# Mixer A's softmax weights of the second layer are turned by VectorE and a round trip through DRAM, and that layer's weights come in halves

## The chip, the cores and the metric

The kernel runs on one core of a Trainium2 chip. The metric is the device time in microseconds of one execution; the median of three runs is 2662.04 us.

## The reference

Two layers of a hybrid encoder over 256 tokens of 2048 channels, in float32. Each layer is, in short:

```python
mod = silu(c) @ ada_w[l] + ada_b[l]                  # six vectors of 2048: shift, scale, gate, twice
h = rmsnorm(x, norm_mix[l]) * (1 + sc_a) + sh_a
qa, ka, va, qb, kb, vb, ga, gb = split_cols(h @ w_in[l])
ya = window_attention(rot(norm(qa)), rot(norm(ka)), va, sink_a[l]) @ w_proj_a[l]   # mixer A, 8 heads
yb = neighbourhood_attention(norm(qb), norm(kb), vb, rel_bias_b[l]) @ w_proj_b[l]  # mixer B, 8 heads
x = x + gt_a * ((sigmoid(ga) * ya + sigmoid(gb) * yb) @ w_out[l])
h = rmsnorm(x, norm_ffn[l]) * (1 + sc_m) + sh_m
g, v = split(depthwise_conv(h @ w_up[l]), 2)
x = x + gt_m * ((silu(g) * v) @ w_down[l])
```

In both mixers a head's softmax weights are a 256 x 256 matrix p (queries by keys). The product with v contracts over the keys, so p has to be turned: keys on the partitions, queries along the row.

## The kernel before

All weights of a layer are one stream of 128 x 128 blocks in the order of their use. Sixteen blocks are a unit of 1 MB; a unit is loaded by SyncE into one of four `raw` tiles, which the modulation weights `aw` share. ScalarE casts each half of a unit to float32r (L336, the high part) and VectorE subtracts that from the original (L337, the low part), into one of four `hl` tiles. TensorE makes three matmuls of each block: high by high, high by low and low by high. `tokens` (L408) makes the q, k, v projections, with L418 to L420; `features` (L392) makes everything else, through `feature_block` (L355 to L357). The list `bg` of background jobs is advanced once at the end of each unit (`tick`, L264); a job has a rate in steps per unit.

The attention of both mixers is such a job (`attention`, L906), at `ATT[l]` steps a unit, and `ATT_B[l]` after mixer A's projection. At each step every live head moves on by one `yield`, and one new head starts if its q and k are there. A head's steps are: scores on TensorE (L648), row maximum, exponential and division on VectorE and ScalarE (L651 to L667); then p is turned and split into high and low parts pT (L430 on ScalarE, L431 on VectorE); then the product with v on TensorE (L697).

There are two ways to turn p. Where `rows` is None, TensorE makes four 128 x 128 transposes into PSUM (`tp`, L689). Otherwise `turned_blocks` (L308) lets VectorE turn each 32 x 32 block in place (L313), into q's and k's own room, and GpSimd's queue writes the blocks to a DRAM tile `pY` at their turned places, eight DMAs of 32 KB a head (L316). `later(BACK[...], back)` reads them back through SyncE's queue, two DMAs of 128 KB (L299), a number of units later, or when the job comes to pT, whichever is first; a read-back is also kept behind the last weight half that VectorE had been given (`BEHIND`). `MOVED[l]` says how many heads of mixer A and of mixer B go this second way: before, none in the first layer, and mixer B's eight in the second. The steps of GpSimd are otherwise the reciprocal roots of the q and k norms (`qrs`, L482) and of the layer norms.

`attended(HA)` runs mixer A's heads to their end before its projection. The instructions of each engine are put in order by a scheduler when the program is built; each engine, and each queue, then runs them in that order.

Of the kernel before, what the change touches and what calls it, by code (L numbers as in the profile page):

```python
# [9 lines left out]
F32 = mybir.dt.float32  # L10
# [5 lines left out]
P = 128  # L16
L = 2
D = 2048
S = 256
# [12 lines left out]
BLOCK = 32  # L32
# [47 lines left out]

H_RATE = [2.7, 1.7]

ATT = [1.288, 0.4]
ATT_B = [0.21, 0.4]

SCORES_3 = (1,)

BACK = [3, 4]
MOVED = [(0, 0), (0, 8)]

ADA_ORDER = [[p * KC + k for k in range(KC) for p in ps] for ps in ((0, 1), (2,), (3, 4), (5,))]
ADA_ORDER = [i for part in ADA_ORDER for i in part]
# [47 lines left out]
def encoder(ctx: ExitStack, tc: tile.TileContext, a: dict, out: bass.AP):  # L140
    nc = tc.nc
# [18 lines left out]
    dram = pool("dram", 2, space=bass.MemoryType.DRAM)  # L160
# [54 lines left out]
    def ada(l):  # L215

        mod = lay.tile([P, 96], F32, name=f"mod{l}", tag="mod")
        ab = load(a["ab"][l], [P, 96], f"ab{l}", lay, tag="ab", bufs=1)
        nrm = load(a["nrm"][l], [P, 2, KC], f"nrm{l}", lay, tag="nrm", bufs=1)
        amod = lay.tile([P, 2, KC], F32, name=f"amod{l}", tag="amod")  # L220
        mods[l], amods[l] = mod, amod
        for n, i in enumerate(ADA_ORDER):
            if l == 0 and n in OWN:
                if OWN[n] not in own:
                    own[OWN[n]] = [place(OWN[n], 16 if OWN[n] == "o" else 12, F32, f"aw_{OWN[n]}"), 0]
                t, k = own[OWN[n]]
                own[OWN[n]][1] += 1
                raw = t[:, KC // 2 * k : KC // 2 * (k + 1)].rearrange("p k s -> p (k s)")
            else:
                raw = rawp.tile([P, D], F32, name=f"aw{l}_{n}", tag="raw")  # L230
            nc.sync.dma_start(raw[:], a["aw"][l, n])
            nc.vector.tensor_tensor_reduce(  # L232
                out=raw[:], in0=raw[:], in1=cact[:], scale=1.0, scalar=ab[:, i : i + 1],
                op0=ALU.mult, op1=ALU.add, accum_out=mod[:, i : i + 1],
            )
            part, kc = divmod(i, KC)
            if part in (1, 4):
                w = part // 3
                nc.vector.scalar_tensor_tensor(
                    out=amod[:, w, kc : kc + 1], in0=mod[:, i : i + 1], scalar=1.0, in1=nrm[:, w, kc : kc + 1],  # L240
                    op0=ALU.add, op1=ALU.mult,
                )
            done[l] = n + 1
            yield
# [42 lines left out]
    def once(fn):  # L287
# [6 lines left out]

        return run

    def read_back(dst, src):

        tc.add_manual_dep(nc.sync.dma_start(dst, src).ins, halved[0], BEHIND)  # L299
# [7 lines left out]

    def turned_blocks(p, rows, n, tag):  # L308

        y = dram.tile([P, n, S], F32, name=tag, tag=tag)  # L310
        to = y[:].rearrange("(b i) n (t a j) -> t a i n b j", i=BLOCK, t=2, a=P // BLOCK)
        for t, row in enumerate(rows):
            nc.vector.transpose(out=row, in_=p[t])  # L313
            src = row.rearrange("p (n b j) -> p n b j", n=n, j=BLOCK)
            for a in range(P // BLOCK):
                nc.gpsimd.dma_start(to[t, a], src[a * BLOCK : (a + 1) * BLOCK])  # L316
        return y

    def unit_steps(l, u, by_halves=False):

        raw = rawp.tile([P, UB * P], F32, name=f"w{l}_{u}", tag="raw")
        if not by_halves:
            nc.sync.dma_start(raw[:], a["ws"][l, u])
        halves = []
        streamed = any(m == "w_in" and mo < GATE_A // P for m, _, mo in STREAMS[l][u * UB : (u + 1) * UB])
        at = OFF if streamed else 0
        for j in range(2):
            n = UB * P // 2  # L330
            hl = hlp.tile([P, 2 * n + ROW], F32R, name=f"hl{l}_{u}_{j}", tag="hl")
            hl = hl[:, at : at + 2 * n].rearrange("p (a n) -> p a n", a=2)
            r = raw[:, j * n : (j + 1) * n]
            if by_halves:
                nc.sync.dma_start(r, a["ws"][l, u][:, j * n : (j + 1) * n])
            nc.scalar.copy(hl[:, 0], r)  # L336
            halved[0] = nc.vector.tensor_tensor(  # L337
                out=hl[:, 1], in0=r, in1=hl[:, 0].bitcast(F32), op=ALU.subtract
            ).ins.name
            halves.append(hl)  # L340
            if j == 0:
                yield halves

    def unit(l, u):
        steps = unit_steps(l, u)
        halves = next(steps)
        for _ in steps:
            pass
        return halves
# [293 lines left out]
    def attend(q, k, v, p, mask, scale, sink, o, rows=None):  # L643

        sc = ax.tile([P, 2, S], F32, name="sc", tag="ax")
        for t in range(2):
            for i, j in by(q):
                nc.tensor.matmul(sc[:, t], q[i][:, t * P : (t + 1) * P], k[j], start=i + j == 0, stop=(i, j) == by(q)[-1])  # L648
        m = sm.tile([P, 2], F32, name="m", tag="m")
        for t in range(2):  # L650
            nc.vector.tensor_tensor_reduce(  # L651
                out=p[:, t], in0=sc[:, t], in1=mask[:, t], scale=scale, scalar=-3.0e38 if sink is None else sink,
                op0=ALU.add, op1=ALU.max, accum_out=m[:, t : t + 1],
            )
        nm = sm.tile([P, 2], F32, name="nm", tag="nm")
        nc.vector.tensor_scalar(out=nm[:], in0=m[:], scalar1=-1.0, scalar2=None, op0=ALU.mult)
        den = sm.tile([P, 2], F32, name="den", tag="den")
        for t in range(2):
            nc.scalar.activation(out=p[:, t], in_=p[:, t], func=AF.Exp, bias=nm[:, t : t + 1], accum_out=den[:, t : t + 1])
        if sink is not None:  # L660
            es = sm.tile([P, 2], F32, name="es", tag="es")
            nc.scalar.activation(out=es[:], in_=nm[:], func=AF.Exp, bias=sink)
            nc.vector.tensor_tensor(out=den[:], in0=den[:], in1=es[:], op=ALU.add)
        ri = sm.tile([P, 2], F32, name="ri", tag="ri")
        nc.vector.reciprocal(out=ri[:], in_=den[:])
        for t in range(2):
            nc.scalar.activation(out=p[:, t], in_=p[:, t], func=AF.Copy, scale=ri[:, t : t + 1])  # L667
        yield
        if rows is not None:
            rows = rows()  # L670
            y = turned_blocks([p[:, t] for t in range(2)], rows, 2, "pY")

            def back():
                for k in range(2):
                    read_back(rows[k], y[:, k])

            back = once(back)
            later(BACK[sink is None], back)
            yield
            yield  # L680
            back()
            pT = at.tile([P, 2, 2, S], F32R, name="pT", tag="pT", bufs=1)
            for k in range(2):
                split(pT[:, :, k], rows[k])
        else:
            tp = ax.tile([P, 2, S], F32, name="tp", tag="ax")
            for k in range(2):
                for t in range(2):
                    nc.tensor.transpose(tp[:, k, t * P : (t + 1) * P], p[:, t, k * P : (k + 1) * P], ident[:])  # L689
            pT = at.tile([P, 2, 2, S], F32R, name="pT", tag="pT", bufs=1)  # L690
            split(pT, tp[:])
        v = v()
        yield
        po = ax.tile([P, 512], F32, name="po", tag="ax")
        for i, j in by(v):
            for b in range(2):
                nc.tensor.matmul(po[:, :S], v[i][:, b], pT[:, j, b], start=i + j + b == 0, stop=i + b == 2)  # L697
        o = o()
        nc.scalar.copy(o[:, 0], po[:, :S])
        nc.vector.tensor_tensor(out=o[:, 1], in0=po[:, :S], in1=o[:, 0].bitcast(F32), op=ALU.subtract)  # L700
# [115 lines left out]
    for l in range(L):  # L816
# [41 lines left out]
        def head_a(i):  # L858
# [18 lines left out]
            def rows():  # L877
# [3 lines left out]
            yield from attend(  # L881
                q, k, v, p, tables[0], SCALE, sink[:, i : i + 1], lambda: oA[i], rows if i < MOVED[l][0] else None
            )

        def head_b(hb):
# [8 lines left out]
                q, k, lambda: in_halves(v[:, :, i * HEAD : (i + 1) * HEAD], f"vB{l}_{hb}", "vh", True), p, p, 1.0, None,  # L894
                lambda: oB_of(hb), (lambda: [b[:, 8 + i], b[:, i]]) if hb < MOVED[l][1] else None,
            )
# [38 lines left out]
        for pi, (groups, gates) in enumerate(parts):  # L935
            last = pi == len(parts) - 1
            for g, part in enumerate(groups):
                have_h(part)
                pss = st.tokens(h, part)
                if pi == max(0, len(parts) - 2) and g == 0:  # L940
                    gains, sink, cw, rots = small(l)
                dst = packs[g // 3][:, 4 * (g % 3) : 4 * (g % 3) + 4]
                rows = dst.rearrange("p (t a) s -> p t (a s)", t=2)
# [25 lines left out]
                if g == 2:  # L969
                    bg.add(job, ATT[l])  # L970

# [29 lines left out]
        for tag in ("y0", "y1", "y2"):  # L1001
            t = place(tag, 4, F32, f"gb{l}_{tag}")
            gb += [t[:, i] for i in range(4)]
        for i in range(2):
            t = paired(F32, f"gb{l}_{i}")
# [56 lines left out]
        for gi, chunks in enumerate(FF_GROUPS):  # L1062
# [34 lines left out]
            for cs in sets:  # L1097
                fns = [lambda p, e=e, c=c: e(p, c) for c in cs for e in (g_evac, v_evac)]
                src = bare.chunks if gi == 0 and cs[0] < BARE[1] // 2 else bare.h
# [113 lines left out]
```

## Time and profile before

| | |
|---|---|
| median of 3 runs | 2662.04 us (2660.14 to 2663.26) |
| profiled execution | 2661.44 us, span 2659.3 us |
| TensorE busy | 2647.6 us (100% of the span) |
| VectorE busy | 2106.2 us (79%) |
| ScalarE busy | 1411.5 us (53%) |
| GpSimd busy | 75.0 us (3%) |
| moved by DMA | 704.63 MB, mean 265 GB/s |
| mixer A of the second layer | scores from 1507.5 us, its last transposes at 1634.2 us |
| mixer B of the second layer | scores from 1634.4 us, its last read-back issued at 1767.3 us |

Times within the execution are counted from the start of the span. PE is TensorE's matmuls and PEld its weight loads, DVE VectorE, ACT ScalarE, POOL GpSimd, SP SyncE; L689 is line 689 of the kernel before. Matmuls are pipelined: their durations overlap, so TensorE's share of busy time does not say how much work it does, and its time is better counted from start to start.

### The profile page before, as it was taken

The page shows a single profiled execution, that of the slowest core. Times are in us where ns is not written, and L with a number is a line of the kernel's source. Part 1 is how long each engine was busy: PE and PEld are TensorE (multiplying, and loading weights), DVE is VectorE, ACT ScalarE, POOL GpSimd, SP SyncE. Part 2 cuts the span into 40 slices and gives each one's busy share as a digit, 9 for nine tenths or more (in the row PEclk, how much of TensorE's full clock was granted, in tenths as well). Part 3 has the DMA queues.
Part 4 walks back from the last instruction along what each step waited for, and adds up shares of the span by engine and source line. Part 5 has one row for each costly group of instructions (what it writes and reads, how often), then busy time and mean ns, then how long its engine had stood idle before and what let it go on. Part 6 is the DMA issues. An engine that isn't in the chain of part 4 may idle for free.

```text
span 2659.3 us, 50973 instructions
## 1 busy us (share of the span) xinstructions
PE 2647.6 (100%) x21224; PEld 2562.6 (96%) x21224; DVE 2106.2 (79%) x2983; ACT 1411.5 (53%) x2292; POOL 75.0 (3%) x89
## 2 busy tenths in 40 slices
PE   9999999999999999999999999999999999999999
PEld 7888899999999999999998889999999999999999
DVE  8898998997987888788876666868888866655664
ACT  5445865456653554355554566555565445544553
POOL 0001100000000000000000001310000000000000
PEclk9999999999999999999999999999999999999999
DMA  9987789885777778788756666877747765555554
GB/s 365 349 327 297 264 300 351 321 311 212 290 295 286 296 290 287 288 297 296 295 205 256 236 229 238 299 264 261 278 179 287 297 251 191 191 197 194 196 191 143
DMA packets 106394, 704.63 MB, mean 265 GB/s; under 512 B 14001, under 2 KB 18353, under 8 KB 22321
## 3 DMA queue, kind: packets, MB, share of 16 engines
q1 hardware_dynamic: 104114, 699.27, 71.6%
q8 instruction: 166, 2.72, 0.4%
q0 software_dynamic: 2048, 2.10, 0.3%
q14 instruction: 66, 0.54, 0.1%
HBM read 697.13 MB, written 4.19 MB: 264 GB/s over the span
## 4 chain that ended last, share of the span: by engine, by line
PE 90%; DVE 5%; DMA 2%; ACT 1%; issue 1%; POOL 0%; DVEq 0%; ACTq 0%
PE ps L355 25%; PE ps L357 25%; PE ps L356 25%; PE ps_t L420 4%; PE ps_t L418 4%; PE ps_t L419 4%; DVE hl L337 2%; DVE aw L232 1%; DMA aw<-in_aw 1%; PE sc L648 1%; PE po L697 1%; ACT hl L336 1%; PE tp L689 0%; PE qtp L621 0%; DMA w<-in_ws 0%
## 5 line engine op out<-in xcount | busy, mean ns | idle before, releaser
L337 DVE TENSOR_TENSOR hl<-w,hl 128x1024 fp32r<-128x1024 f32 x928 | 1128.4, 1222 | 338.7 <-ACT hl L336 332.1
L336 ACT CAST hl<-w 128x1024 fp32r<-128x1024 f32 x928 | 970.6, 1049 | 738.3 <-PE ps L357 509.5
L355 PE MATMUL ps<-h,hl 128*128 128x256 f32 x3328 | 923.9, 278 | 1.3 <-DVE ya L979 0.6
L356 PE MATMUL ps<-h,hl 128*128 128x256 f32 x3328 | 921.1, 277 | 0.0
L357 PE MATMUL ps<-h,hl 128*128 128x256 f32 x3328 | 920.9, 277 | 0.0
L355 PEld LDWEIGHTS ps<-h,hl 128*128 128x128 f32 x3328 | 625.0, 188 | 2.4 <-DVE ya L979 0.8
L356 PEld LDWEIGHTS ps<-h,hl 128*128 128x128 f32 x3328 | 625.6, 188 | 0.4
L357 PEld LDWEIGHTS ps<-h,hl 128*128 128x128 f32 x3328 | 624.6, 188 | 0.0
L232 DVE CUSTOM_DVE_ANT_0 aw<-aw,cact,ab 128x2048 f32<-128x2048 f32 x189 | 443.5, 2347 | 61.1 <-DMA aw<-in_aw 60.4
L418 PE MATMUL ps_t<-hl,h 128*128 128x512 f32 x576 | 223.5, 393 | 2.1 <-ACT h L510 1.6
L419 PE MATMUL ps_t<-hl,h 128*128 128x512 f32 x576 | 225.1, 391 | 0.4
L420 PE MATMUL ps_t<-hl,h 128*128 128x512 f32 x576 | 224.6, 391 | 0.0
L1058 DVE SCALAR_TENSOR_TENSOR u<-ps,cw,u 128x255 f32<-128x255 f32 x304 | 146.2, 481 | 66.5 <-ACT u L1056 62.5
L1056 ACT ACTIVATE u<-ps,cw 128x256 f32<-128x256 f32 x152 | 85.7, 564 | 183.1 <-PE ps L357 183.0
L357 PE MATMUL ps<-merged,hl 128*128 128x256 f32 x512 | 141.8, 277 | 0.2 <-DVE hl L337 0.2
L355 PE MATMUL ps<-merged,hl 128*128 128x256 f32 x512 | 141.7, 277 | 0.0
L356 PE MATMUL ps<-merged,hl 128*128 128x256 f32 x512 | 141.7, 277 | 0.0
L356 PE MATMUL ps<-act_o,hl 128*128 128x256 f32 x512 | 141.6, 277 | 0.0
L357 PE MATMUL ps<-act_o,hl 128*128 128x256 f32 x512 | 141.6, 276 | 0.0
L355 PE MATMUL ps<-act_o,hl 128*128 128x256 f32 x512 | 141.4, 277 | 0.0
L418 PEld LDWEIGHTS ps_t<-hl,h 128*128 128x128 f32 x576 | 108.0, 188 | 25.5 <-ACT h L510 2.6
L419 PEld LDWEIGHTS ps_t<-hl,h 128*128 128x128 f32 x576 | 108.2, 188 | 24.0 <-DVE hl L337 2.1
(235 smaller groups left out, 4657.8 us busy)
## 6 DMA issues: line engine op xcount, KB each, us to landing
w<-in_ws SPq DMA_DIRECT2D x463, 1024.0 KB, 5.0
aw<-in_aw SPq DMA_DIRECT2D x189, 1024.0 KB, 6.1
p<-in_bias SPq DMA_DIRECT2D x16, 256.0 KB, 4.4
x<-in_xT SPq DMA_DIRECT2D x4, 512.0 KB, 5.5
aw_o<-in_aw SPq DMA_DIRECT2D x2, 1024.0 KB, 13.1
pY<-packB POOLq DMA_DIRECT2D x64, 32.0 KB, 4.2
packB<-pY SPq DMA_DIRECT2D x16, 128.0 KB, 2.7
out<-x SPq DMA_DIRECT2D x16, 128.0 KB, 2.6
```

The costliest lines, as they stand in the source:

```text
L232: nc.vector.tensor_tensor_reduce(out=raw[:], in0=raw[:], in1=cact[:], scale=1.0, scalar=ab[:, i : i + 1], op0=ALU.mult, op1=ALU.add, accum ...
L336: nc.scalar.copy(hl[:, 0], r)
L337: halved[0] = nc.vector.tensor_tensor(out=hl[:, 1], in0=r, in1=hl[:, 0].bitcast(F32), op=ALU.subtract).ins.name
L355: nc.tensor.matmul(out, hi, act[0], start=first, stop=False)
L356: nc.tensor.matmul(ps[:, :S], hi, act[1], start=False, stop=False)
L357: nc.tensor.matmul(out, lo, act[0], start=False, stop=last)
L418: nc.tensor.matmul(ps[:], xh, hi, start=kc == kcs[0], stop=False)
L419: nc.tensor.matmul(ps[:], xh, lo, start=False, stop=False)
L420: nc.tensor.matmul(ps[:], xl, hi, start=False, stop=kc == kcs[-1])
L648: nc.tensor.matmul(sc[:, t], q[i][:, t * P : (t + 1) * P], k[j], start=i + j == 0, stop=(i, j) == by(q)[-1])
L1056: nc.scalar.activation(out=u, in_=ps, func=AF.Identity, scale=w[:, 1:2], bias=w[:, 3:4])
L1058: nc.vector.scalar_tensor_tensor(out=u[:, to], in0=ps[:, of], scalar=w[:, j : j + 1], in1=u[:, to], op0=ALU.mult, op1=ALU.add)
```

## The change

- `MOVED[1]`: all eight heads of mixer A in the second layer now go the second way, by VectorE's block transposes (into q's room and a spare tile), GpSimd's queue, DRAM and SyncE's queue.
- `turned_blocks` returns its DMAs as a list, and `by_gpsimd` issues the eight of them after both block transposes.
- `ATT[1]`: the second layer's attention runs at 0.46 steps a unit instead of 0.4 until mixer A's projection is done.
- `BACK`: a read-back is made 3 units after the block transposes in both mixers (mixer B's was 4). The number of steps between the block transposes and pT is now written as `STEPS`, with the same value 2.
- Weights: the first 76 units of the second layer's stream (up to mixer B's projection) are loaded in two halves of 512 KB each, and so are all 96 rows of its modulation weights, of which the first half or so are loaded during the first layer.

```diff
-ATT = [1.288, 0.4]
+ATT = [1.288, 0.46]
 ATT_B = [0.21, 0.4]
...
-BACK = [3, 4]
-MOVED = [(0, 0), (0, 8)]
+BACK = [3, 3]
+STEPS = [2, 2]
+SMALL = 76
+MOVED = [(0, 0), (8, 8)]
...
-            nc.sync.dma_start(raw[:], a["aw"][l, n])
+            for part in range(1 + l):
+                cols = slice(part * D // (1 + l), (part + 1) * D // (1 + l))
+                nc.sync.dma_start(raw[:, cols], a["aw"][l, n][:, cols])
...
+    def by_gpsimd(outs):
+
+        for to, src in outs:
+            nc.gpsimd.dma_start(to, src)
+
...
-        y = dram.tile([P, n, S], F32, name=tag, tag=tag)
+        y, outs = dram.tile([P, n, S], F32, name=tag, tag=tag), []
         to = y[:].rearrange("(b i) n (t a j) -> t a i n b j", i=BLOCK, t=2, a=P // BLOCK)
         for t, row in enumerate(rows):
             nc.vector.transpose(out=row, in_=p[t])
             src = row.rearrange("p (n b j) -> p n b j", n=n, j=BLOCK)
-            for a in range(P // BLOCK):
-                nc.gpsimd.dma_start(to[t, a], src[a * BLOCK : (a + 1) * BLOCK])
-        return y
+            outs += [(to[t, a], src[a * BLOCK : (a + 1) * BLOCK]) for a in range(P // BLOCK)]
+        return y, outs
...
     def unit(l, u):
-        steps = unit_steps(l, u)
+        steps = unit_steps(l, u, l == 1 and u < SMALL)
...
-            y = turned_blocks([p[:, t] for t in range(2)], rows, 2, "pY")
+            y, outs = turned_blocks([p[:, t] for t in range(2)], rows, 2, "pY")
+            by_gpsimd(outs)
...
             later(BACK[sink is None], back)
-            yield
-            yield
+            for _ in range(STEPS[sink is None]):
+                yield
             back()
```

## The prediction

> **What bounds the kernel now.** I read the page first, then the engines' busy time by stage, then TensorE's and GpSimd's timelines around mixer A and mixer B of the second layer.
>
> From the page (span, TensorE, and the chain that ended last, by engine):
> ```profile
> span 2659.3 us, 50973 instructions
> PE   2647.6 (100%) x21224; PEld 2562.6 (96%) x21224; DVE 2106.2 (79%) x2983; ACT 1411.5 (53%) x2292; POOL 75.0 (3%) x89
> PE 90%; DVE 5%; DMA 2%; ACT 1%; issue 1%; POOL 0%; DVEq 0%; ACTq 0%
> ```
> Stages of 20 us in the second layer, busy us of each engine: mixer A beside q/k/v (1520 to 1640), mixer B beside A's projection (1660), and the merge (1820):
> ```profile
> core 0: us, PE busy (x) PEld busy (x) DVE busy (x) ACT busy (x) POOL busy (x), PEclk, DMA share, GB/s
> 1520.00:1540.00 20.00, 20.00 (x99) 16.89 (x98) 13.80 (x22) 13.32 (x35) 1.64 (x1) 1.00 0.64 245
> 1620.00:1640.00 20.00, 19.94 (x175) 19.73 (x174) 13.80 (x24) 13.53 (x28) 0.00 (x0) 1.00 0.76 282
> 1660.00:1680.00 20.00, 20.00 (x176) 20.00 (x176) 17.77 (x36) 12.38 (x25) 6.73 (x12) 1.00 0.80 260
> 1820.00:1840.00 20.00, 20.00 (x177) 20.00 (x177) 19.62 (x32) 9.87 (x14) 0.00 (x0) 1.00 0.75 279
> ```
> TensorE is busy throughout, at full granted clock, even where VectorE has 19.62 of 20 us. What the other two engines wait for, in 1560 to 1600 (groups of ScalarE, then of VectorE):
> ```profile
> L336 ACT CAST hl<-w 128x1024 fp32r<-128x1024 f32 x14 | 14.7, 1047 | 11.0 <-PE ps_t L420 11.0
> ```
> ```profile
> L337 DVE TENSOR_TENSOR hl<-w,hl 128x1024 fp32r<-128x1024 f32 x14 | 17.0, 1224 | 10.9 <-ACT hl L336 10.9
> L232 DVE CUSTOM_DVE_ANT_0 aw<-aw,cact,ab 128x2048 f32<-128x2048 f32 x2 | 4.7, 2350 | 2.9 <-DMA aw<-in_aw 2.9
> ```
> The casts of the weights wait for TensorE (11.0 us of idle time, no load in it), and VectorE waits for the casts. So TensorE sets the pace, and the four half tiles hl are the store ahead of it. Fourteen halves in 40 us are 2.85 us a half, 5.7 us a unit; with one half in use, three lie ahead: about 8.5 us. Only work taken off TensorE is a gain here, and a wait elsewhere costs nothing until it outlasts that store.
>
> **The change part by part.** *Removed from TensorE:* 8 heads x 4 transposes. TensorE's timeline at one head beside q/k/v, then at the one beside the gates:
> ```profile
> 1519.00 0.39 PE L420 MATMUL ps_t<-hl,h 128*128 128x512 f32 x1
> 1519.23 0.60 PE L689 MATMUL tp<-ident,p 128*128 128x128 f32 x4
> 1519.59 0.96 PE L648 MATMUL sc<-kA,qA 128*128 128x256 f32 x6
> 1520.38 0.40 PE L418 MATMUL ps_t<-hl,h 128*128 128x512 f32 x1
> ```
> ```profile
> 1633.33 0.28 PE L356 MATMUL ps<-h,hl 128*128 128x256 f32 x1
> 1633.44 0.28 PE L357 MATMUL ps<-h,hl 128*128 128x256 f32 x1
> 1633.78 0.66 PE L689 MATMUL tp<-ident,p 128*128 128x128 f32 x4
> 1634.19 0.37 PE L355 MATMUL ps<-h,hl 128*128 128x256 f32 x1
> ```
> The second layer's 32 by themselves, duration in ns (min, median, max):
> ```profile
> L689 PE MATMUL tp<-ident,p x32: 270/272/327, 1519.2 to 1634.2; 128*128 128x128 f32 x32
> ```
> Durations overlap, so I count from start to start. The four hold TensorE from 1519.23 to 1519.59, 0.36 us; by the spacing inside the group, (0.60 - 0.27) / 3 = 0.11 us each, it is 0.44. At 1633.44 the next projection matmul comes 0.75 us later instead of 0.11, so this head costs 0.64. Sum: 7 x 0.36 + 0.64 = 3.2, or 7 x 0.44 + 0.64 = 3.7; I take 3.4 us.
>
> *Moved on TensorE:* the scores and products go into the stream of weights at other places. In the built programs they interrupt the q/k/v matmuls at eight places before and at eleven after, since a head's scores no longer stand beside its predecessor's transposes. One interruption costs, beyond its matmuls, 1520.38 - 1519.59 = 0.79 less 6 x 0.113 (the L356 to L357 step) = 0.68: 0.11 us. Three more make +0.3 us. The gain is 3.1 us.
>
> *Added on VectorE, removed there:* these groups of the whole run:
> ```profile
> L313 DVE STREAM_TRANSPOSE packB<-p 128x256 f32<-128x256 f32 x16 | 6.4, 430 | 1.7 <-ACT p L667 1.7
> L431 DVE TENSOR_TENSOR pT<-packB,pT 128x256 fp32r<-128x256 f32 x16 | 6.0, 419 | 0.0
> L431 DVE TENSOR_TENSOR pT<-tp,pT 128x512 fp32r<-128x512 f32 x24 | 16.4, 685 | 0.8 <-ACT pT L430 0.8
> ```
> Per head 2 x 0.430 + 2 x 0.419 - 0.685 = 1.01 us, 8.1 us in all, over the 23 units (131 us) from the first block transposes to the last pT of mixer A: 6% on a VectorE at 13.80 of 20. The pace 0.46 instead of 0.4 steps a unit packs 15% more attention into a unit; the densest place, A's projection with mixer B (17.77 of 20), should rise to about 18.5. That is under the 19.62 at which TensorE still ran without a gap. Cost 0; without that cover, at most the 8.1 us.
>
> *Added on GpSimd's queue:* 64 issues of 32 KB, 8 a head, queued ahead of mixer B's own 64 and between the rsqrt steps (qrs) that q/k normalisation needs. Mixer B shows the rate (first head; then two heads; one qrs):
> ```profile
> 1613.91 1.64 POOL L482 TENSOR_TENSOR qrs<-qss,mhalf 128x8 f32<-128x8 f32 x1 [48.83 <-DVE qss L481]
> 1640.91 2.00 POOL L316 DMA_DIRECT2D pY<-packB  x3 [25.36 <-DVE packB L313]
> 1644.42 1.83 POOL L316 DMA_DIRECT2D pY<-packB  x3 [1.52 <-issue]
> 1650.43 1.33 POOL L316 DMA_DIRECT2D pY<-packB  x2 [4.18 <-issue]
> ...
> 1702.54 1.83 POOL L316 DMA_DIRECT2D pY<-packB  x3 [5.57 <-DVE packB L313]
> ...
> 1727.77 0.61 POOL L316 DMA_DIRECT2D pY<-packB  x1 [3.38 <-issue]
> ```
> A head takes 10.9 us (1640.91 to 1651.76), or 12.9 where VectorE is fuller (1702.54 to 1728.38, two heads), far more than 8 x 0.61: issues come in threes and then pause. A new head comes every 1 / 0.46 = 2.17 units, 12.4 us (14.3 before). It fits, barely. A qrs behind four such issues comes some 4 us later; VectorE's qn waits that long with the next weight halves behind it, three times, each inside the 8.5 us store.
>
> *Added on SyncE's queue:* 16 read-backs, and 172 more loads, since the second layer's 96 modulation weights and the first 76 units come in two halves. Sizes and times to landing, an example in SyncE's timeline, and who waited for it:
> ```profile
> w<-in_ws SPq DMA_DIRECT2D x463, 1024.0 KB, 5.0
> pY<-packB POOLq DMA_DIRECT2D x64, 32.0 KB, 4.2
> packB<-pY SPq DMA_DIRECT2D x16, 128.0 KB, 2.7
> w<-in_ws SPq DMA_DIRECT2D x2, 512.0 KB, 12.4
> ```
> ```profile
> 1655.24 0.33 SPq L231 DMA_DIRECT2D aw<-in_aw  x1
> 1660.70 0.81 SPq L299 DMA_DIRECT2D packB<-pY  x2
> 1661.62 2.49 SPq L325 DMA_DIRECT2D w<-in_ws  x2
> ```
> ```profile
>   ACT pT L430: 1.1, 1
> ```
> An issue is 0.33 us; a unit then has some four of them, well inside 5.7 us. A half should land in about the 5.0 us of a whole; the ends are 2.7 (the 128 KB read-back) and 12.4 (the two halves at the kernel's start). Even at 12.4 the load is 7.4 us later, less than the 8.5 us store. The sum of a modulation row (L232) needs both halves; the second is issued 0.33 us later, which lengthens VectorE's 2.9 us of idle time above, not TensorE's. Cost 0.
>
> *The new wait:* pT of mixer A waits for its read-back, on ScalarE (cast) and VectorE (subtract), with the next weight halves queued behind on both; on SyncE the next weight loads are queued behind the read-back. A head's read-back is due 3 units (17 us) after its block transposes, its pT two steps (24.8 us) after. Writing takes 10.9 + 4.2 = 15.1 us, the read-back 2.7. Mixer B's first read-back left SyncE at 1660.70 after a pause of 5 us and its pT waited 1.1 us; TensorE had 20.00 of 20 in that stage. I take 0 for mixer A; the ends are 0 and the rival below.
>
> *Mixer B's part:* its read-backs are due after 3 units instead of 4, its pT still after two steps (24.8 us at 0.46, 28.5 at 0.4 once A's projection is done), and its heads come some units sooner because of the pace. All eight issues of a head now follow both block transposes, so the first four start 0.43 us later. SyncE may stand a little longer at L299, as at 1660.70. Cost 0 by the same stage, within the same rival.
>
> **The sum.** 2661.44 us (the profiled execution's time; span 2659.3) - 3.4 + 0.3 = **2658.3 us**. The median of the runs, 2662.04, stands 0.6 above that execution. With the bounds 3.7 and 2.6 (3.2 less twice 0.3) and the runs' own spread (2660.14 to 2663.26), this case holds 2656 to 2661. A difference of 0.2%, 5.3 us, is about what a measurement of this kernel can tell from no change, so the gain falls within it.
>
> **The rivals.** *GpSimd's queue falls behind (slower).* Sixteen heads now follow each other through it without a pause. If a head takes 13.8 us, as it may where VectorE is near 18 of 20, the queue loses 1.4 us a head, 22 us, and three qrs of 1.64 add 5. SyncE then stands at the read-back, weight loads start late, and pT blocks ScalarE and VectorE. The first 2 us (17 - 15.1) and the 8.5 us store are free; TensorE waits for the other 16.5: 2661.44 - 3.1 + 16.5 = 2674.8. It decides from 12.9 us a head, where the loss (0.5 x 16 + 5 = 13, less 10.5) eats the gain; a middle of 13.4 gives 2668.4. For it: 12.9 was seen. Against it: 10.9 was seen where VectorE had about 14 of 20, as in mixer A, and a stalled VectorE lets GpSimd catch up. Chance 0.2.
>
> *VectorE locks GpSimd out.* Descriptors would be written only while VectorE is idle: at 13.80 of 20 that leaves 6.2 us in 20 against 8 x 0.61 x 20 / 12.4 = 7.9. Short by 1.7 us in 20, 11 us over mixer A's 131; less 10.5 that is 0.5, 2658.8 us, and nothing is left of the difference. The trace speaks against it:
> ```profile
> 1640.82 2.31 DVE L232 CUSTOM_DVE_ANT_0 aw<-aw,cact,ab 128x2048 f32<-128x2048 f32 x1
> ```
> Three issues ran from 1640.91 to 1642.91, inside VectorE's instruction with two inputs. Chance 0.04. The Trainium skill ("SBUF — State Buffer", SBUF: two separate sides) has this as a rule: the port pair that the two engines share is locked for a whole instruction, and a DMA issued by GpSimd starves while VectorE holds it. By that rule the change would be hurt most where VectorE is fullest; the three issues beside L232 do not bear it out.
>
> *The halves speed up the queue (faster).* The pauses of GpSimd's queue would shrink, but nothing waits for them on TensorE, which has 20.00 of 20. More than the transposes' 3.7 us can't come off; over 5.3 only by the runs' spread. Chance 0.05. The Trainium skill ("DMA: Bandwidth & Descriptors", Queues, rings and completion order) says that a DMA engine changes between queues packet by packet; by that, rows of 4 KB in place of 8 KB shorten the turn that a small write waits, which speaks against the first rival.
>
> *The change does nothing there:* ruled out; in the built program the 32 transposes are gone.
>
> **How the numbers follow.** Forecast 0.71, GpSimd's queue behind 0.2, locked out 0.04 (no change), halves 0.05. Of the forecast's 0.71, 0.02 may turn slower by a wait that I don't see and 0.01 faster by the runs' spread. Slower by over 0.2%: 0.2 + 0.02 = 0.22; faster 0.05 + 0.01 = 0.06; within 0.68 + 0.04 = 0.72. The range goes from 2655.5, the forecast's low end less half a us, to 2667.5, about half of the queue's case.
>
> **What would show it.** Right: tp of the second layer gone; TensorE at 20.00 of 20 from 1500 to 1800; 16 more block transposes near 0.43 us; heads through GpSimd's queue in 9 to 12.4 us; TensorE's span shorter by 3 us at the end of mixer A and by as much at the end. Wrong: waits of TensorE for hl between 1500 and 1800, pT waiting for its read-back by more than 8 us, SyncE standing at L299 with casts that wait for w, or a VectorE at 20 of 20 in A's projection.

## The result, and the profile after

The changed kernel takes 2729.22 us (median of 6 runs, 2716.52 to 2736.19), the kernel before 2662.05 us beside it: a ratio of 1.0241, interval 1.0215 to 1.0268 (the quotient of the two medians is 1.0252). The forecast was 2658.3 us in a range of 2655.5 to 2667.5. It is wrong in sign, and the time lies 62 us above the range.

From the page of the changed kernel (span, TensorE's busy time, the chain that ended last by engine, and the costliest group that changed):

```profile
span 2727.3 us, 51466 instructions
PE 2668.9 (98%) x21192; PEld 2573.7 (94%) x21192; DVE 2107.5 (77%) x3007; ACT 1401.4 (51%) x2300; POOL 114.4 (4%) x153
PE 54%; DMA 20%; DVE 14%; issue 8%; ACT 2%; SPq 1%; POOL 1%; DVEq 0%; ACTq 0%; POOLq 0%
L236 DVE CUSTOM_DVE_ANT_0 aw<-aw,cact,ab 128x2048 f32<-128x2048 f32 x189 | 443.9, 2349 | 206.8 <-DMA aw<-in_aw 205.9
```

The 32 matmuls of the transposes are gone (21224 to 21192), and yet TensorE's share of the chain fell from 90% to 54%. What came in is DMA, 20%. The last row is the sum over one modulation row (L232 before), 189 times in the whole execution: VectorE now idles 205.9 us for these loads to land. Before it was 60.4:

```profile
L232 DVE CUSTOM_DVE_ANT_0 aw<-aw,cact,ab 128x2048 f32<-128x2048 f32 x189 | 443.5, 2347 | 61.1 <-DMA aw<-in_aw 60.4
```

**Where the time went**, by three landmarks: the matmuls of A's projection, of B's projection and of the last FFN product, from the operations of one tile. The last number of "first to last start" is the second layer's. Before, then after:

```profile
L357 PE MATMUL ps<-oA,hl x256: 274/277/468, 339.0 to 1704.6; 128*128 128x256 f32 x128
L357 PE MATMUL ps<-oB,hl x256: 275/277/279, 490.0 to 1842.6; 128*128 128x256 f32 x128
L357 PE MATMUL ps<-act_o,hl x512: 275/277/280, 780.7 to 2653.9; 128*128 128x256 f32 x171
```

```profile
L365 PE MATMUL ps<-oA,hl x256: 276/276/581, 338.1 to 1761.3; 128*128 128x256 f32 x128
L365 PE MATMUL ps<-oB,hl x256: 276/276/278, 489.1 to 1902.7; 128*128 128x256 f32 x128
L365 PE MATMUL ps<-act_o,hl x512: 276/276/420, 781.3 to 2722.1; 128*128 128x256 f32 x171
```

It is 56.7 us late at the end of A's projection, 60.1 at the end of B's, 68.2 at the end. But most was lost before the attention whose code was changed had begun: in the first layer's FFN, where the second layer's modulation rows are loaded. This is that stage, 880 to 1300 us, before and after:

```profile
880.00:1300.00 420.00, 420.00 (x3695) 420.00 (x3694) 352.70 (x461) 213.14 (x292) 0.00 (x0) 1.00 0.80 293
```

```profile
880.00:1300.00 420.00, 401.86 (x3437) 396.08 (x3436) 322.99 (x424) 189.46 (x270) 0.00 (x0) 1.00 0.77 270
```

In the same 420 us TensorE made 3437 matmuls instead of 3695, at a granted clock of 1.00 in both: 258 x 0.114 us (420 / 3695) = 29 us lost. The first write of the second layer's attention on GpSimd shows the loss up to there, in the changed kernel and in move_alone (below), which has the same attention and whole modulation rows:

```profile
1548.42 2.01 POOL L304 DMA_DIRECT2D pY<-packA  x3 [15.91 <-DVE spare L322]
```

```profile
1507.96 2.01 POOL L302 DMA_DIRECT2D pY<-packA  x3 [15.92 <-DVE spare L320]
```

So 40.5 of the 68 us are lost before the first write of the attention.

**The loop.** SyncE's and VectorE's timelines, before and then after:

```profile
959.40 0.33 SPq L231 DMA_DIRECT2D aw<-in_aw  x1
...
955.49 2.35 DVE L232 CUSTOM_DVE_ANT_0 aw<-aw,cact,ab 128x2048 f32<-128x2048 f32 x1 [0.80 <-DMA aw<-in_aw]
966.38 2.35 DVE L232 CUSTOM_DVE_ANT_0 aw<-aw,cact,ab 128x2048 f32<-128x2048 f32 x1 [0.77 <-DMA aw<-in_aw]
```

```profile
956.69 0.33 SPq L333 DMA_DIRECT2D w<-in_ws  x1
958.22 0.80 SPq L235 DMA_DIRECT2D aw<-in_aw  x2
...
954.30 2.35 DVE L236 CUSTOM_DVE_ANT_0 aw<-aw,cact,ab 128x2048 f32<-128x2048 f32 x1 [3.79 <-DMA aw<-in_aw]
966.32 2.35 DVE L236 CUSTOM_DVE_ANT_0 aw<-aw,cact,ab 128x2048 f32<-128x2048 f32 x1 [2.17 <-DMA aw<-in_aw]
```

The sum over a row ends (956.65), its `raw` tile is free, and SyncE issues the next unit into it (956.69). The next half of weights is subtracted, which frees another tile, and the next row's load goes out (958.22). It lands, and the sum over it starts at once (966.32). From one sum to the next row's issue it takes 3.91 us before and 3.92 after; from that issue to the next sum 6.98 before and 8.10 after. Together 10.89 and 12.02 us, in which TensorE gets two units of weights and needs 10.9 us for them. The turn had next to no slack: a row that lands later delays the next weight load and the next row's issue, and so each row adds to the lateness of the one before.

### The profile page after: what moved, and what is told of

The parts are those of the page before. It is cut to its first block, busy times and chain, and to the rows that moved or that the text cites. A ratio compares the mean times of both kernels' runs of the same rounds, so it can differ in the third digit from the quotient of the medians.

```text
span 2727.3 us, 51466 instructions
## 1 busy us (share of the span) xinstructions
PE 2668.9 (98%) x21192; PEld 2573.7 (94%) x21192; DVE 2107.5 (77%) x3007; ACT 1401.4 (51%) x2300; POOL 114.4 (4%) x153
## 4 chain that ended last, share of the span: by engine, by line
PE 54%; DMA 20%; DVE 14%; issue 8%; ACT 2%; SPq 1%; POOL 1%; DVEq 0%; ACTq 0%; POOLq 0%
DMA aw<-in_aw 19%; PE ps L365 14%; PE ps L363 14%; PE ps L364 13%; DVE hl L345 6%; PE ps_t L427 4%; PE ps_t L426 4%; PE ps_t L428 4%; DVE aw L236 3%; ACT hl L344 1%; DVE u L1067 1%; SPq L235 1%; PE sc L656 1%; POOL pY L304 1%; PE po L706 0%
## 5 line engine op out<-in xcount | busy, mean ns | idle before, releaser
L236 DVE CUSTOM_DVE_ANT_0 aw<-aw,cact,ab 128x2048 f32<-128x2048 f32 x189 | 443.9, 2349 | 206.8 <-DMA aw<-in_aw 205.9
```

The costliest lines, as they stand in the source:

```text
L236: nc.vector.tensor_tensor_reduce(out=raw[:], in0=raw[:], in1=cact[:], scale=1.0, scalar=ab[:, i : i + 1], op0=ALU.mult, op1=ALU.add, accum ...
```

## The experiments

**Which part costs what.** Four kernels. *before_aw_halves* and *before_unit_halves* add one kind of halves to the kernel before; *aw_whole* takes the modulation rows' halves out of the changed kernel, and *move_alone* those of the units too, which leaves mixer A's move with its pace and due times.

```diff
 # before_aw_halves (before_unit_halves: unit_steps(l, u, l == 1 and u < 76) alone)
-            nc.sync.dma_start(raw[:], a["aw"][l, n])
+            for part in range(1 + l):
+                cols = slice(part * D // (1 + l), (part + 1) * D // (1 + l))
+                nc.sync.dma_start(raw[:, cols], a["aw"][l, n][:, cols])
 # aw_whole: the changed kernel with the "-" line in place of the "+" lines
 # move_alone: aw_whole with
-SMALL = 76
+SMALL = 0
```

> The kernel before with one edit: the second layer's modulation rows come in two halves of 512 KB. Theory 1: 38 us in the first layer and 8 in the second's feed-forward part, and up to 10 in the attention: 2708 to 2718. Theory 2: 2662, as nothing in GpSimd's queue changes.

> The kernel before with one edit: the first 76 units of the second layer come in two halves of 512 KB. Theory 1: 2662 within 3, since a unit's first half can be cast while the second lands, and casts wait for TensorE. A third theory, that every halved load costs: 10 us or more.

> The changed kernel with one edit: the second layer's modulation rows come whole (1 MB) again; the units' halves, the move of mixer A and the pace stay. Theory 1 (the load loop): VectorE's sum of a modulation row, the load that takes the freed tile and the next sum form a loop that runs at TensorE's pace without slack, and the second half's later landing lengthens it by about 1 us a row. Then TensorE's extra gaps of the first layer (38 us more than before between 900 and 1400) and of the second layer's feed-forward part (8 us) vanish, and 2661 to 2684 us are left, by how much of the 25 us lost in the attention is theirs as well. Theory 2 (GpSimd's queue alone costs): the time stays near 2729.

> The changed kernel with every load whole again: only the move of mixer A, its pace 0.46 and the read-backs after 3 units are left. Theory 1: no loss outside the attention; inside it VectorE still waits twice some 5 us for a root behind GpSimd's write issues, so between 2659 (the store of halves hides them) and 2670. Theory 2: the attention's 25 us stay, 2684. The packet rule (rows of 8 KB delay the small writes) has it slower than the run with the units in halves by some us.

| kernel | median, us | ratio to before | interval |
|---|---|---|---|
| before_aw_halves | 2708.31 | 1.0179 | 1.0162 to 1.0196 |
| before_unit_halves | 2660.65 | 1.0001 | 0.9992 to 1.0010 |
| aw_whole | 2673.36 | 1.0049 | 1.0034 to 1.0064 |
| move_alone | 2665.80 | 1.0019 | 1.0009 to 1.0028 |

The halves of the modulation rows alone cost 47.6 us of the 67, by ratio times 2661; the units' halves alone nothing that can be told from no change; the move alone 5 us where 3 were to be gained. The units' halves cost 7.6 us once the move is there (aw_whole against move_alone). VectorE's groups in 880 to 1300 us of before, and of before_aw_halves:

```profile
L337 DVE TENSOR_TENSOR hl<-w,hl 128x1024 fp32r<-128x1024 f32 x154 | 187.4, 1220 | 29.8 <-ACT hl L336 29.8
L232 DVE CUSTOM_DVE_ANT_0 aw<-aw,cact,ab 128x2048 f32<-128x2048 f32 x40 | 94.0, 2350 | 32.7 <-DMA aw<-in_aw 32.6
```

```profile
L339 DVE TENSOR_TENSOR hl<-w,hl 128x1024 fp32r<-128x1024 f32 x140 | 169.8, 1218 | 8.9 <-ACT hl L338 8.9
L234 DVE CUSTOM_DVE_ANT_0 aw<-aw,cact,ab 128x2048 f32<-128x2048 f32 x37 | 87.0, 2352 | 93.8 <-DMA aw<-in_aw 93.8
```

The wait for a row grows from 0.82 us (32.7 / 40) to 2.54 (93.8 / 37), and 14 halves of weights fewer get through, 14 x 2.73 us = 38 us. VectorE's program is the same instruction for instruction in both.

So is TensorE's, and the start of a matmul can be set beside that of the same matmul in before. The first row in halves is issued at 834.71 us. TensorE is still level (0.3 us late) at 877 us of before, 1.6 us late at 887, 7.8 at 955 and 45.7 at 1347: the store covers about the first five rows, and then each row costs about 1 us.

Three stretches of TensorE's time, one profiled execution each: up to the last FFN product of the first layer (last start of act_o there), from there to the end of B's projection, and from there to the last FFN product:

| kernel | first layer, us | second layer to B's projection | rest |
|---|---|---|---|
| before | 1346.2 | 496.4 | 811.3 |
| before_aw_halves | 1391.9 | 496.3 | 813.6 |
| move_alone | 1345.9 | 503.9 | 811.3 |
| aw_whole | 1345.4 | 509.5 | 811.2 |
| the changed kernel | 1386.4 | 516.3 | 819.4 |

The rows' halves by themselves cost nothing beside the attention (496.3). The 19.9 us that the changed kernel loses there are 7.5 of the move, 5.6 of the units' halves and 6.8 of the rows' halves, each added to the one before (one execution each; that of move_alone is 2.5 us above its median).

**What it is about the halves.** Halves by columns have pieces of 4 KB instead of 8 KB (theory 1a), and are two DMAs (theory 1b). Three versions of the load in the kernel before (of each, only the lines that say what is loaded where; in the first two they stand in the loop over `part`, and all three apply to the second layer):

```diff
 # before_aw_rows: two DMAs of 64 neighbouring partitions, rows of 8 KB
+                ps = slice(part * P // (1 + l), (part + 1) * P // (1 + l))
+                nc.sync.dma_start(raw[ps], a["aw"][l, n][ps])
 # before_aw_alt: two DMAs, even and odd partitions, rows of 8 KB
+                to = raw[:].rearrange("(q t) d -> t q d", t=2)[part]
+                nc.sync.dma_start(to, a["aw"][l, n].rearrange("(q t) d -> t q d", t=2)[part])
 # before_aw_4k: one DMA, two pieces of 4 KB a partition (the host lays the second layer's rows out so)
+                to = raw[:].rearrange("p (h c) -> p h c", h=2)
+                nc.sync.dma_start(to, a["aw"][l, n].rearrange("(h q) (t c) -> (q t) h c", h=2, t=2))
```

> The kernel before with the second layer's modulation rows in two loads of 512 KB by partitions: 64 partitions with rows of 8 KB each, instead of 128 with rows of 4 KB. The load loop of 10.9 us a row stands; the question is what lengthens it. Theory 1a (the rows of 4 KB start slowly after rows of 8 KB; the packets of the halves ran at 12 to 20 in half a microsecond before they reached 45): with rows of 8 KB the loss of 47.6 us goes, 2661 to 2670. Theory 1b (a second load costs its own issue and completion): the loss stays, 2700 to 2712.

> Kernel before, with each modulation row of the second layer in two loads, one of the even partitions and one of the odd ones, in whole rows of 8 KB. Theory 1a (size of the pieces): 2660 to 2664 us. Theory 1b (a second DMA): 2700 to 2712 us, landing of the second 7.5 us after the first one's issue. If packets take 600 ns or more, as in the two loads of 64 neighbouring partitions, it is near 2730 us and says nothing on 1a and 1b.

> Kernel before, with each modulation row of the second layer still loaded by one DMA of 1 MB, but in 256 pieces of 4 KB instead of 128 rows of 8 KB (the host lays the rows out accordingly). Theory 1a, the size of the pieces alone makes a row land late: issue to landing 7.5 us instead of 6.6, VectorE waits some 2.5 us a row from 880 to 1300 us, 2700 to 2712 us. Theory 1b, it is the second DMA (its issue 0.4 us later, its own start behind the first): landing 6.6 us, wait 0.3 to 0.8 us a row, 2660 to 2664 us.

Measured: before_aw_rows 2730.61 us (1.0256, 1.0239 to 1.0272), before_aw_alt 2715.44 (1.0192, 1.0172 to 1.0212), before_aw_4k 2667.91 (1.0018, 1.0005 to 1.0031). The first met neither theory's number. In 880 to 1300 us of before_aw_alt VectorE has these groups:

```profile
L342 DVE TENSOR_TENSOR hl<-w,hl 128x1024 fp32r<-128x1024 f32 x139 | 165.6, 1219 | 13.0 <-ACT hl L341 13.0
L237 DVE CUSTOM_DVE_ANT_0 aw<-aw,cact,ab 128x2048 f32<-128x2048 f32 x36 | 84.4, 2344 | 0.0
L1063 DVE SCALAR_TENSOR_TENSOR u<-ps,cw,u 128x255 f32<-128x255 f32 x107 | 51.4, 480 | 53.5 <-ACT u L1061 52.5
```

Its rows are never waited for (0.0). It loses a like time in another way: the scheduler that builds the program put the sums elsewhere when the load was split by partitions. In the traces 798 of VectorE's 2983 instructions stand at other places than in before, and a sum now follows the convolution step (L1063), which waits for TensorE's own results, with the next weights queued behind. before_aw_rows has that same order. So a time near 1b's came out of before_aw_alt by another mechanism (its second half landed 5.2 us after the first one's issue, where 1b expected 7.5), and the times of these two runs do not tell 1a from 1b. before_aw_4k does better, since VectorE's order there is that of before:

```profile
L341 DVE TENSOR_TENSOR hl<-w,hl 128x1024 fp32r<-128x1024 f32 x154 | 187.2, 1219 | 17.2 <-ACT hl L340 17.0
L236 DVE CUSTOM_DVE_ANT_0 aw<-aw,cact,ab 128x2048 f32<-128x2048 f32 x39 | 91.7, 2352 | 52.3 <-DMA aw<-in_aw 52.3
```

Pieces of 4 KB in one DMA raise the wait to 1.34 us a row (52.3 / 39), as many halves of weights get through that stage (154 again), and the run is 4.8 us longer by its ratio, a little above 1b's 2664 and far below 1a's 2700. The longer wait came out of VectorE's other idle time, for the casts (29.8 us before, 17.2 here, 8.9 in before_aw_halves): this was the slack that the loop had. So theory 1a falls as the main cause.

Theory 1b is not shown by that. Medians in 880 to 1300 us, first of before_aw_halves, then of before_aw_alt:

```profile
aw<-in_aw SPq DMA_DIRECT2D x72, 512.0 KB, 7.0
```

```profile
aw<-in_aw SPq DMA_DIRECT2D x70, 512.0 KB, 4.6
```

From the first issue to the landing of both halves it is 7.5 us in before_aw_halves and 5.2 in before_aw_alt, while a whole row takes 6.6 in before and 7.1 in before_aw_4k. So two DMAs with rows of 8 KB do not land late (though the loads stand at other places there); as far as these runs show, it takes the second DMA and the pieces of 4 KB together. Of the later landing 0.38 us is the second issue (958.22 and 958.60 in the changed kernel); why the rest comes from the two together stays open. In before_aw_rows, whose halves are 64 neighbouring partitions each, both have landed after 10.5 us, and 27% of the 8 KB packets of that stage take 600 ns or more (6% in before): its time is a third case.

**What the move itself costs.** Three versions of move_alone, against the theory that a qrs stands behind writes for which GpSimd's queue has no room:

```diff
 # move_ring: twice the room for GpSimd's descriptors (the space is taken from one of three z tiles)
-    nc = _bacc.Bacc("TRN2", target_bir_lowering=False, num_devices=1, dynamic_dma_scratch_size=1024)
+    nc = _bacc.Bacc("TRN2", target_bir_lowering=False, num_devices=1, dynamic_dma_scratch_size=2048)
 # move_act_queue: the writes go by ScalarE's queue
-            nc.gpsimd.dma_start(to, src)
+            nc.scalar.dma_start(to, src)
 # move_pace_42: a slower pace of the attention
-ATT = [1.288, 0.46]
+ATT = [1.288, 0.42]
```

> The move of mixer A alone (all loads whole) with GpSimd's descriptor memory at 2048 instead of 1024 bytes a partition; to make room, the scratch tiles z have two buffers instead of three. Theory 2a (three writes in flight fill the memory; the fourth waits for a landing, and a root behind it makes VectorE wait 6 us): six or more issues go without a pause, a head takes 6 to 9 us instead of 11.8, VectorE's waits of 6.0 and 5.7 us for a root fall below 3, TensorE's gaps in the attention fall from 6.7 to under 2 us: 2657 to 2661. If the pauses come from VectorE's lock, nothing changes: 2665.

> The move of mixer A alone with the block writes issued by ScalarE's queue instead of GpSimd's. Theory 2 (GpSimd's queue is what costs): the roots come at once, SyncE's read-backs wait less, and TensorE keeps the 3.1 us: 2657 to 2660. Against it, 8 issues a head of some 0.35 us stand among ScalarE's casts, behind the block transposes: if ScalarE then waits for VectorE, 2662 to 2670.

> The move of mixer A alone at 0.42 steps a unit instead of 0.46: a head every 13.6 us instead of 12.4. Theory 2 (GpSimd's queue is full at 11 to 13.7 us a head): the queue gets pauses, read-backs are less late, 2660 to 2664. If the pace is not the point: 2665 to 2667.

GpSimd in move_alone, the qn that waits for it on VectorE, and GpSimd in move_ring:

```profile
1536.48 1.83 POOL L302 DMA_DIRECT2D pY<-packA  x3 [4.51 <-DVE spare L320]
1542.46 0.61 POOL L302 DMA_DIRECT2D pY<-packA  x1 [4.15 <-issue]
1543.10 1.67 POOL L488 TENSOR_TENSOR qrs<-qss,mhalf 128x8 f32<-128x8 f32 x1
...
1544.79 0.69 DVE L603 TENSOR_TENSOR qn<-ps_t,qrs 128x512 f32<-128x512 f32 x1 [5.99 <-POOL qrs L488]
```

```profile
1506.60 2.61 POOL L302 DMA_DIRECT2D pY<-packA  x4 [15.92 <-DVE spare L320]
1509.21 2.58 POOL L302 DMA_DIRECT2D pY<-spare  x4
...
1534.30 2.43 POOL L302 DMA_DIRECT2D pY<-packA  x4 [10.54 <-DVE spare L320]
1536.85 1.66 POOL L488 TENSOR_TENSOR qrs<-qss,mhalf 128x8 f32<-128x8 f32 x1
```

With 1024, three writes go out and the fourth waits 4.15 us for nothing that an engine does: it goes at 1542.46, when the first has landed (1542.16). By issue and landing times, never more than three of the 128 writes are in flight in move_alone, and up to seven in move_ring, where eight go out in 5.2 us without a pause. The median is 2660.43 us (0.9992, 0.9982 to 1.0001), 5.4 us under move_alone's. So the limit is how many writes fit, not how fast GpSimd writes descriptors. (With two z tiles the scheduler also put 198 of VectorE's 3007 instructions at other places; what that is worth by itself no run shows.) ScalarE's queue is worse: 2695.78 us (1.0125, 1.0108 to 1.0142); TensorE then waits for ScalarE's casts, which stand in order behind the issues (the two rows are among TensorE's waits there, and make 8.6 of the 30 us that it is above move_alone):

```profile
PE ps_t L424 <- ACT hl L342: 4.5, 4, 2.2
PE ps L361 <- ACT hl L342: 4.1, 7, 1.4
```

move_pace_42 missed: 2682.97 us (1.0080, 1.0065 to 1.0095) where 2660 to 2664 had been expected. TensorE's two long waits there, and VectorE before the first:

```profile
1626.28 0.55 PE L361 MATMUL ps<-h,hl 128*128 128x256 f32 x1 [6.01 <-DVE qn L603]
1676.22 0.58 PE L362 MATMUL ps<-oA,hl 128*128 128x256 f32 x1 [5.22 <-DVE oA L707]
...
1625.44 1.29 DVE L603 TENSOR_TENSOR qn<-ps_t,qrs 128x512 f32<-128x512 f32 x2 [6.60 <-POOL qrs L488]
```

At the slower pace the last head of mixer A isn't finished when its projection needs it (oA). And a qn that waits 6.60 us holds TensorE for 6.01: here the store of weights covered nothing, because the next matmul waits for qn itself.

**Do the units' halves cost anything without that limit, and can the rest of the wait go?** *ring_unit_halves* is move_ring with `SMALL = 76`. *move_ring_plan* is move_ring with the modulation rows of this stage asked for around the end of mixer A:

```diff
-ADA_PLAN_1 = [(8, 143), (76, 166), (84, 168), ...]
+ADA_PLAN_1 = [(8, 143), (34, 156), (60, 158), (76, 166), (84, 168), ...]
```

> The changed kernel with the modulation rows whole, twice the room for GpSimd's descriptors (2048) and two z tiles instead of three: move_ring with the first 76 units in halves. Theory 2, unit halves cost something (7.5 us, aw_whole against move_alone) only because they delay the small writes behind which GpSimd's queue of three stands: with room for more writes 2660 to 2663 us. Rival, the halves delay the modulation rows and read-backs themselves in this stage, whatever GpSimd's queue does: 2666 to 2670 us.

> move_ring, with fewer modulation rows asked for beside the attention's crowded end (rows 143 to 156 by unit 34, 156 to 158 by unit 60, 158 to 166 by unit 76, instead of an even 143 to 166). If what is left of TensorE's waits in move_ring (0.47 and 2.87 us) comes from VectorE standing at a late modulation row, they go and the time is 2657 to 2659 us; if the rows only move the wait elsewhere, 2660 to 2662 us.

ring_unit_halves does not decide. Its median is 2664.04 us and its ratio 1.0003 (0.9989 to 1.0017), but five of its ten runs lie at 2657.2 to 2661.3 us, theory 2's value or less, and five at 2666.8 to 2669.5, the rival's. The profiled execution is one of the five short ones; there the stretch to B's projection takes 496.8 us, against 498.2 in move_ring, so the units' halves cost nothing in it. Of a long one there is no trace. move_ring_plan has the lowest median: 2658.06 us, ratio 0.9986 (0.9974 to 0.9997); the interval overlaps move_ring's, so what the plan adds is not shown by the times. TensorE's matmuls of A's projection, 1640 to 1720 us, in move_ring and then in move_ring_plan:

```profile
L363 PE MATMUL ps<-oA,hl 128*128 128x256 f32 x128 | 36.4, 285 | 2.9 <-DVE hl L343 2.9
```

```profile
L363 PE MATMUL ps<-oA,hl 128*128 128x256 f32 x128 | 35.5, 277 | 0.0
```

The 2.9 us wait was VectorE standing at a late modulation row, and it is gone.

The execution that was profiled is itself a long one, 2664.26 us, and shows how near its limit the loop of the first layer is. With whole rows, in 680 to 1300 us, TensorE makes 5369 matmuls there instead of 5446 in move_ring's, some 9 us less work; a row lands in 7.1 us instead of 6.6 (medians), and VectorE waits 98.1 us for the rows instead of 10.8. The same loop falls behind in one execution and not in another.

## Why the prediction was wrong, step by step

- **The step that failed: the halves of a modulation row, "cost 0".** The prediction let the second half be "issued 0.33 us later, which lengthens VectorE's 2.9 us of idle time, not TensorE's". VectorE's idle time did lengthen (60.4 to 205.9 us), but the sum over a row also frees the tile for the next load. The prediction looked at one load against a store of 8.5 us; it is a loop, and its lateness adds up. The store was used up after about five rows, and every later row cost TensorE about 1 us. It cost 47.6 us alone. The sign was in the page of before: the sums idled 60.4 us for their loads, 32.6 of them in 880 to 1300 us, so that their load, and not VectorE, ended the turn there; and about half of the second layer's rows are loaded beside the first layer's FFN, a stage that the prediction did not examine.
- **"A half should land in about the 5.0 us of a whole"** was roughly right for the units and asked the wrong question for the rows. The changed kernel's DMA issues:

```profile
w<-in_ws SPq DMA_DIRECT2D x387, 1024.0 KB, 5.0
aw<-in_aw SPq DMA_DIRECT2D x192, 512.0 KB, 6.4
w<-in_ws SPq DMA_DIRECT2D x154, 512.0 KB, 5.6
```

  A half of a unit lands in 5.6 us, longer than a whole in 5.0, and half of a row in 6.4. The Trainium skill ("Perfetto Trace Analysis", DMA Optimizations) says that splitting a DMA may let some of it start sooner, and that the whole may complete sooner if the DMA engines are generally idle. Here their share was 0.80 in the rows' stage, and the consumer needs both halves; splitting gained nothing.
- **Transposes -3.4, interruptions +0.3: right, as far as one execution shows.** In the stretch from the first layer's last FFN product to the end of B's projection, move_ring_plan's TensorE waits for nothing and takes 492.7 us, against 496.4 in before: 3.7 us off, where 3.1 were forecast.
- **VectorE's added work: right.** The block transposes and subtractions of mixer A in 1540 to 1800 us of the changed kernel:

```profile
L322 DVE STREAM_TRANSPOSE packA<-p 128x256 f32<-128x256 f32 x8 | 3.5, 440 | 0.6 <-ACT p L675 0.6
L439 DVE TENSOR_TENSOR pT<-spare,pT 128x256 fp32r<-128x256 f32 x8 | 3.4, 419 | 0.0
L438 ACT CAST pT<-packA 128x256 fp32r<-128x256 f32 x8 | 3.3, 418 | 1.7 <-DMA packA<-pY 1.7
```

  They take 0.44 and 0.42 us, as the rows of before said. The new wait, pT for its read-back, is the last row: 1.7 us on ScalarE in all, where 0 was taken.
- **GpSimd's queue: the rate was read rightly, the verdict "it fits, barely" was too kind.** The pauses after three issues were seen and not followed to their cause. In move_alone a head takes 7.3 to 14.6 us, and VectorE's qn waits up to 5.99 us instead of some 4. The move alone cost 5.0 us instead of gaining 3.1: the first rival's kind, at a middle size (its middle case was 2668.4 us, by its own terms 2668.8; measured 2665.8). Its way was in part another. Of the 6.7 us that TensorE waits in 1500 to 1800 us of move_alone, 1.6 come right after VectorE's waits for qrs, 2.5 are a head's scores waiting for ScalarE, and 2.6 come after VectorE stood at a late modulation row. Such rows make VectorE wait 28.7 us there and 8.6 in before. In move_ring the first two kinds are gone and 2.9 us of the third are left. The qn of 1500 to 1740 us in before, in move_alone and in move_ring:

```profile
L597 DVE TENSOR_TENSOR qn<-ps_t,qrs 128x512 f32<-128x512 f32 x6 | 3.9, 686 | 5.4 <-POOL qrs L482 5.4
```

```profile
L603 DVE TENSOR_TENSOR qn<-ps_t,qrs 128x512 f32<-128x512 f32 x6 | 3.9, 686 | 11.6 <-POOL qrs L488 11.6
```

```profile
L603 DVE TENSOR_TENSOR qn<-ps_t,qrs 128x512 f32<-128x512 f32 x6 | 3.9, 684 | 3.0 <-POOL qrs L488 3.0
```

  In the changed kernel SyncE stood at the read-backs as well, 23.5 and 16.8 us for the writes:

```profile
SPq L308 <- DMA pY<-spare: 23.5, 14, 6.1
SPq L308 <- DMA pY<-packB: 16.8, 9, 5.7
```

- **VectorE locks GpSimd out: not borne out.** In move_ring GpSimd issues eight writes in 5.2 us beside VectorE's work, with twice the room for descriptors and one z tile less. The Trainium skill's rule ("SBUF — State Buffer", SBUF: two separate sides) has pauses that end with VectorE's instructions; the pause of 4.15 us shown above ended with a landing, and VectorE was idle all through it (from 1538.81 to 1544.79).
- **The halves speed up the queue: they did not.** pY's writes land in 4.05 us in the changed kernel (median of all 128), 4.2 before. The packet-by-packet turns of the Trainium skill ("DMA: Bandwidth & Descriptors", Queues, rings and completion order) give no gain that shows.

## What to carry to other kernels

Before a load is called hidden, ask what its consumer sets free: if the consumer's end lets the next load start, the path is a loop, its slack is that of one turn, and a store of finished work covers a delay once, not each turn. A group in the profile whose idle time is ended by its own load, turn after turn, may be such a loop near its limit, even while TensorE is at 100%. Look for it in every stage that shares the code that is edited, not only in the stage that the edit is meant for.

## What the runs showed of the hardware that was not expected

- GpSimd's queue had at most three 32 KB writes in flight with descriptor room of 1024 (in move_alone, the fourth waited 4.15 us) and at most seven with 2048 (in move_ring). Doubling it was worth 5.4 us to the move, by the medians.
- A 1 MB load split by columns into two DMAs landed about 1 us later (6.6 us whole, 7.5 for both halves), one DMA with the same 4 KB pieces 0.5 us later (7.1), and two DMAs of even and odd partitions with rows of 8 KB sooner (5.2, with the loads at other places in the order). Two of 64 neighbouring partitions took 10.5 us.
- The way a load is split can change the order of another engine's instructions where a scheduler builds the program: 51 us in before_aw_alt (ratio 1.0192), with no wait of VectorE for that load in the stage shown.
